# A stated order for ScalarE and VectorE in layer zero's attention, and softmax in two steps

## The chip, the cores and the metric

The kernel runs on one core of one Trainium2 chip. The metric is the device time of one execution in microseconds (us). Five engines run beside each other, each through its own list of instructions in order, and they meet at semaphores: TensorE (PE in the profile; its weight loads are PEld), VectorE (DVE), ScalarE (ACT), GpSimd (POOL) and SyncE (SP), whose queue issues the transfers.

## The reference, cut to what matters

A decoder trunk of two layers on 256 tokens of width 1024 (two tiles of 128 tokens). Each layer mixes, then runs a dense feed-forward part (FFN).

```
xn = rms_norm(h, norm_mix[i]);  mn = rms_norm(mem, norm_mem[i])
q, k, v, qm = split(xn @ w_in[i])        # 12 self heads of 64, 4 memory heads
mk, mv = split(mn @ w_mem_kv[i])
self_out = softmax(q k^T / 8 + bias, causal) v   # layer 0: F[t] - F[s], layer 1: ALiBi
mem_out  = softmax(qm mk^T / 8) mv
h = h + concat(self_out, mem_out) @ w_out[i]
h = h + (silu(gate) * up) @ w_down[i]            # of rms_norm(h, norm_ffn[i])
```

In layer 0 F is the running sum of log sigmoid(gate) of each head. With 256 tokens the block selection of layer 1 has no past block, so its heads are causal attention with ALiBi. A last RMSNorm ends it. What the code calls layer 0 is called layer zero below; the change's own words call it layer one.

## The kernel before, in words

All weights come from one stream in the order of use, in units of up to 1 MB, through four `raw` buffers. Each product is computed to near float32 precision from two parts: ScalarE copies half a unit to `hi` in a reduced format (L224) and VectorE subtracts it from the original to give `lo` (L227), a *weight split*; then three matmuls (`prod`, L317) sum hi·hi, lo·hi and hi·lo. There are seven `hi` and seven `lo` buffers. `weights` (L233) asks for a half and has splits emitted up to five halves ahead (`AHEAD`). Activations get the same treatment (`split_ps`, L242: a *head split* where it is a head's output `x_hT`).

A planner at build time orders each engine's instructions by priority, which is the order of emission, and takes the first that its model of the machine has ready. Inside `tc.manual_schedule(engines=...)` the named engines keep the order of emission; where a region's instructions fall among others of the same engine stays the planner's choice. The whole body (L773) is such a region for PE and SP. For ACT and DVE only the v products of layer 0 are (L479), and a last part of layer 1.

A mixer (L466) runs the v products, then three rounds g of queries and keys (`qk_ps`, 96 matmuls each, two pairs of heads a round). Ahead of round 1 come the memory heads (`memory_heads`, L552): in layer 0 first the memory's keys and values (`mem_kv`, L340: products mk and mv, then the spread of the memory's RMS factors over the partitions, `rsb_ps_mem`), then the queries qm. Then the output products `o_acc` follow, in four pieces. The memory's factors need a square over each tile of mem (`factor`, L257: ScalarE `junk_mem` at L254, VectorE, GpSimd); these are emitted in `mem_kv` after its fourth product (L359).

Attention itself is woven in. `attend` (L393) is a generator for a pair of heads; `step()` (L460) moves every live one on to its next `yield`. A step is called after every second k of a round, in mem_kv, in the middle of qm, and ahead of each group of twelve output matmuls. For one pair the stages are: some idle steps (`IDLE`); in one step the bias adds (L543, layer 0), the scores `s` (8 matmuls), the maxima (L415 with the bias for causal heads, called a causal pass here; L418 for memory heads), the exponentials (L425), the reciprocal (L426) and the scaling (L429); two steps later for memory heads, three for causal ones, the transposes `pT` (L436) and their copies (L439 ScalarE, L440 VectorE); two steps later `o` and the head split.

Counted from the first in mem_kv, the steps of layer 0 are: 1 to 4 in mem_kv, 5 in qm, 6 to 9 in round 1, 10 to 13 in round 2, 14 to 19 in the output products, 20 to 22 behind them. With m00 and m01 the memory pairs and s00 to s05 the causal ones, scores come in step 7 (m00), 8 (s00 and m01), 9 (s01), 12 (s02), 13 (s03), 16 (s04), 17 (s05); transposes in step 9 (m00), 10 (m01), 11, 12, 15, 16, 19, 20 (s00 to s05). Matmul outputs go to eight PSUM banks in rotation, and a stage waits until a bank is read out. Probabilities and their transposes share the tag `probs` with three buffers; the two tiles of mem use it at the start.

The change and the prediction's steps touch attend, mixer, mem_kv, the FFN's `spread` (L669) and the tiles of mem (L163).

## Time and profile before

| | |
|---|---|
| median of 3 runs | 624.39 us (624.07 to 624.49) |
| profiled execution | 623.77 us, span 622.0 us |
| mean granted TensorE clock | 0.998 |
| TensorE busy | 608.5 us, 98% of the span |
| VectorE, ScalarE busy | 455.8 us, 392.4 us |

The span goes from the first to the last instruction of the profiled execution. A busy time counts overlapping instructions once. Waits of an engine are marked with what ended them, which is inferred from semaphores; the end of a matmul is modelled.

### The profile page before, as it was taken

To read this page: it belongs to the slowest core of one execution; us is meant where nothing else is said; L and a number is where in the kernel's file an instruction comes from. 1 tells how busy PE (TensorE), PEld (TensorE's weight loads), DVE (VectorE), ACT (ScalarE), POOL (GpSimd) and SP (SyncE) were. 2 spreads that over 40 slices of the span, in tenths; PEclk is the share of its full clock that TensorE was granted. 3 is DMA by queue.
4 is the path that set the end of the run, shared out by engine and by line. 5 is a ranking of instruction groups with operands and counts; after the bars stand their busy time and mean duration, and the time that the engine had idled before them with its cause. 6 is when DMAs were issued, how large, how long until landed. Compare 5 with 4: busy or idle time off the path is not lost.

```text
span 622.0 us, 9564 instructions
## 1 busy us (share of the span) xinstructions
PE 608.5 (98%) x3640; PEld 533.9 (86%) x3640; DVE 455.8 (73%) x827; ACT 392.4 (63%) x737; POOL 61.6 (10%) x90
## 2 busy tenths in 40 slices
PE   8999999999999999999999999999999999999995
PEld 6999887788888888888899999877888888888884
DVE  5677999978677676678675679986867666666664
ACT  7879788575555555557467589865755555555542
POOL 2023122046000000000011032200000000000000
PEclk9999999999999999999999999999999999999999
DMA  8977431525455545555455642332455555555301
GB/s 354 420 276 273 169 136 69 202 96 214 174 195 204 193 173 184 194 203 190 165 187 203 243 144 89 136 135 99 155 191 199 204 188 173 184 199 203 136 1 67
DMA packets 16774, 112.31 MB, mean 181 GB/s; under 512 B 1996, under 2 KB 2008, under 8 KB 4312
## 3 DMA queue, kind: packets, MB, share of 16 engines
q1 hardware_dynamic: 16440, 111.42, 49.1%
q8 instruction: 28, 0.46, 0.3%
q10 hardware_dynamic: 288, 0.29, 0.1%
q14 instruction: 18, 0.15, 0.1%
HBM read 110.64 MB, written 1.06 MB: 180 GB/s over the span
## 4 chain that ended last, share of the span: by engine, by line
PE 81%; DVE 9%; ACT 7%; issue 1%; DMA 1%; SPq 0%; POOLq 0%; POOL 0%; DVEq 0%
PE gu L180 40%; PE d_acc L180 18%; PE qk_ps L180 6%; PE o_acc L180 5%; PE v_ps L180 5%; DVE lo L227 2%; ACT hi L224 2%; DMA raw<-in_stream 1%; PE s_s L180 1%; PE mv_ps L180 1%; PE qm_ps L180 1%; PE mk_ps L180 1%; DVE p_s L415 1%; PE o_s L180 1%; DVE p_s L429 1%
## 5 line engine op out<-in xcount | busy, mean ns | idle before, releaser
L227 DVE TENSOR_TENSOR lo<-raw,hi 128x1024 fp32r<-128x1024 f32 (+3 forms) x201 | 241.0, 1206 | 69.1 <-ACT hi L224 63.8
L224 ACT ACTIVATE hi<-raw 128x1024 fp32r<-128x1024 f32 (+3 forms) x201 | 206.4, 1035 | 73.5 <-PE d_acc L180 47.0
L180 PE MATMUL gu<-x_ffn,hi 128*128 128x512 f32 x704 | 177.5, 392 | 0.0
L180 PEld LDWEIGHTS gu<-x_ffn,hi 128*128 128x128 f32 x704 | 126.3, 189 | 22.2
L180 PE MATMUL d_acc<-hi,h 128*128 128x512 f32 x348 | 107.1, 389 | 0.0
L180 PEld LDWEIGHTS gu<-x_ffn,lo 128*128 128x128 f32 x704 | 96.7, 190 | 8.1 <-ACT x_ffn L248 1.0
L180 PE MATMUL gu<-x_ffn,lo 128*128 128x256 f32 x704 | 100.5, 284 | 0.1
L180 PEld LDWEIGHTS d_acc<-hi,h 128*128 128x128 f32 x348 | 65.3, 188 | 13.6
L180 PE MATMUL qk_ps<-x_x,hi 128*128 128x256 f32 x384 | 72.4, 284 | 0.9 <-ACT p_m L425 0.9
L180 PE MATMUL d_acc<-lo,h 128*128 128x512 f32 x174 | 67.7, 389 | 0.0
L180 PEld LDWEIGHTS qk_ps<-x_x,hi 128*128 128x128 f32 x384 | 60.9, 191 | 1.9 <-ACT p_m L425 1.1
L180 PE MATMUL qk_ps<-x_x,lo 128*128 128x256 f32 x192 | 54.3, 283 | 0.0
L675 ACT ACTIVATE gate<-gu 128x256 f32<-128x256 f32 x44 | 16.9, 384 | 57.6 <-PE gu L180 57.6
L180 PE MATMUL o_acc<-hi,x_hT 128*128 128x512 f32 x128 | 41.7, 405 | 0.5 <-DVE x_hT L246 0.5
L675 ACT ACTIVATE up<-gu 128x256 f32<-128x256 f32 x44 | 16.9, 385 | 39.6 <-PE gu L180 39.4
L180 PEld LDWEIGHTS d_acc<-lo,h 128*128 128x128 f32 x174 | 32.7, 188 | 6.7
L676 DVE TENSOR_TENSOR gate<-gu,gate 128x256 f32<-128x256 f32 x44 | 18.6, 423 | 25.5 <-ACT gate L675 25.5
L180 PEld LDWEIGHTS qk_ps<-x_x,lo 128*128 128x128 f32 x192 | 36.8, 191 | 0.0
L676 DVE TENSOR_TENSOR up<-gu,up 128x256 f32<-128x256 f32 x44 | 18.7, 424 | 24.6 <-ACT up L675 24.6
L180 PE MATMUL v_ps<-hi,x_x 128*128 128x384 f32 (+1 forms) x128 | 33.2, 339 | 0.1
L425 ACT ACTIVATE p_s<-p_s,nmax_s 128x128 f32<-128x128 f32 (+1 forms) x48 | 21.3, 445 | 11.4 <-DVE nmax_s L415 11.4
L180 PEld LDWEIGHTS o_acc<-hi,x_hT 128*128 128x128 f32 x128 | 22.7, 188 | 6.2 <-DVE x_hT L246 1.2
(155 smaller groups left out, 753.7 us busy)
## 6 DMA issues: line engine op xcount, KB each, us to landing
raw<-in_stream SPq DMA_DIRECT2D x94, 1024.0 KB, 4.8
raw<-in_stream SPq DMA_DIRECT2D x3, 1036.0 KB, 7.8
raw<-in_stream SPq DMA_DIRECT2D x4, 768.0 KB, 5.1
fk<-fd SPq DMA_DIRECT2D x3, 512.0 KB, 7.1
raw<-in_stream SPq DMA_DIRECT2D x2, 518.0 KB, 4.2
h<-in_x SPq DMA_DIRECT2D x2, 512.0 KB, 11.9
mem<-in_mem SPq DMA_DIRECT2D x2, 512.0 KB, 12.8
gfin<-in_norm_final SPq DMA_DIRECT2D x1, 512.0 KB, 3.5
```

The source lines that it names most:

```text
L180: nc.tensor.matmul(o, lhsT, rhs, start=self.fresh, stop=stop, skip_group_check=True)
L224: nc.scalar.activation(hi[:, c0:c1], src[:, c0:c1], AF.Copy)
L227: nc.vector.tensor_sub(lo[:, c0:c1], src[:, c0:c1], hi[:, c0:c1].bitcast(F32))
L415: nc.vector.tensor_tensor_reduce(pr[:, a, c], sb[a].t[:, c], more[qt][:, a], scale=-1.0, scalar=-NEG, op0=ALU.add, op1=ALU.min, accum_out= ...
L425: nc.scalar.activation(pr[:, a, c], src, AF.Exp, bias=nmax[:, a, j], scale=scale, accum_out=total[:, a, j])
L429: nc.vector.tensor_scalar_mul(pr[:, a, c], pr[:, a, c], rc[:, a, qt:qt + 1])
L675: nc.scalar.activation(v[:, 1], b[s].t[:, S:], AF.Copy)
L676: nc.vector.tensor_add(v[:, 0], b[s].t[:, :S], v[:, 1])
```

## The change

Five edits:

1. In layer 0 rounds 1 and 2 of queries and keys, each with the steps it calls and the scaling and splitting of queries and keys behind it, and then the output products up to the last step are regions in which ACT and DVE keep the order of emission. The memory heads between are not. Layer 1 stays with the planner.
2. In attend (both layers) the bias is emitted one step earlier, and the reciprocal with the scaling one step later than the exponentials (that step is taken from the ones before the transposes). One reciprocal over four columns replaces two over two.
3. Softmax, the copies of transposes and the head splits get a priority of 75 places (`URGENT`) ahead of their place of emission. Inside the new regions the order of emission holds all the same.
4. The memory's factors are emitted behind round 0, ahead of the x spread, not in mem_kv.
5. `probs` has four buffers, and the FFN's spread factor shares the buffer of the mixer's (tag `x` for `f`).

```diff
+URGENT = 75
-    mem_t = [ap.tile([P, 2, 512], F32, tag="probs", name=f"mem{t}", bufs=3)...
+    mem_t = [ap.tile([P, 2, 512], F32, tag="probs", name=f"mem{t}", bufs=4)...
...
-                if i == 0 and k == 3:
-                    rs_mem.extend(factor(mem_t[t], f"mem{t}") for t in range(NT))
...
-        for _ in range(idle):
+        for _ in range(idle - 1):
             yield
         if causal:
             more = bias(h0)
+        yield
         sb = [bank(f"s_{name}_{a}") for a in range(2)]
...
+        with tc.high_priority(offset=URGENT):
             for a in range(2):
                 for qt in range(NT):
...                 # maxima (L415, L418)
             for a in range(2):
                 for qt in range(NT):
...                 # exponentials (L425)
-            nc.vector.reciprocal(rc[:, a], total[:, a])
-            for qt in range(NT):
-                c = slice(qt * S, qt * S + nk[qt] * P)
-                nc.vector.tensor_scalar_mul(pr[:, a, c], pr[:, a, c], rc[:, a, qt:qt + 1])
-        for _ in range(SOFTMAX_STEPS[causal]):
+        yield
+        with tc.high_priority(offset=URGENT):
+            nc.vector.reciprocal(rc.rearrange("p a t -> p (a t)"), total.rearrange("p a t -> p (a t)"))
+            for a in range(2):
+                for qt in range(NT):
+                    c = slice(qt * S, qt * S + nk[qt] * P)
+                    nc.vector.tensor_scalar_mul(pr[:, a, c], pr[:, a, c], rc[:, a, qt:qt + 1])
+        for _ in range(SOFTMAX_STEPS[causal] - 1):
             yield
...
+        with tc.high_priority(offset=URGENT):
             nc.scalar.activation(pT[:, 0, :width], tb[0].t[:, :width], AF.Copy)
             nc.vector.tensor_copy(pT[:, 1, :width], tb[1].t[:, :width])
...
+        with tc.high_priority(offset=URGENT):
             split_ps(dst[0][:, kt, :], dst[1][:, kt, :], ob.t[:, :S])
...
         for g in range(3):
             if g == MEM_AT[i]:
                 memory_heads()
+            with tc.manual_schedule(engines={ACT, DVE}) if g >= MEM_AT[i] and i == 0 else nullcontext():
                 kb = [bank(f"qk_ps{i}{2 * g + a}") for a in range(2)]
...             # the round's products, with a step() behind every second k
+                if i == g == 0:
+                    rs_mem.extend(factor(mem_t[t], f"mem{t}") for t in range(NT))
                 if g == 0:
                     rsb = spread(rs, f"x{i}", (DH ** -0.5, 1.0), "x")
...             # queries and keys of two pairs, their attend() started
+        with tc.manual_schedule(engines={ACT, DVE}) if i == 0 else nullcontext():
             acc = [[bank(f"o_acc{i}{t}{c}") for c in range(2)] for t in range(NT)]
...
             for n, j in enumerate((3, 0, 1)):
                 for kk in range(2):
                     step()
                     for t in range(NT):
                         o_item(n, j, kk, t)
             while active:
                 step()
...
-                rsb.append(spread(rs, f"f{i}", (1.0,), "f")[:, 0])
+                rsb.append(spread(rs, f"f{i}", (1.0,), "x")[:, 0])
```

## Rows read from the trace of the kernel before

**Rows 1.** From the page: the span, and busy time, share and instructions of each engine.

```profile
span 622.0 us, 9564 instructions
...
PE 608.5 (98%) x3640; PEld 533.9 (86%) x3640; DVE 455.8 (73%) x827; ACT 392.4 (63%) x737; POOL 61.6 (10%) x90
```

**Rows 2.** Busy time by stretch: the stretch and its length, then busy us and, in brackets, instructions of PE, PEld, DVE, ACT and POOL in this order, the granted clock of TensorE, the share of time in which the DMA engines are busy, and GB/s.

```profile
24.00:62.00 38.00, 37.11 (x305) 36.12 (x304) 29.00 (x41) 33.45 (x63) 8.93 (x9) 1.00 0.77 300
62.00:124.00 62.00, 59.03 (x408) 49.94 (x407) 60.08 (x174) 45.49 (x119) 10.02 (x16) 1.00 0.39 144
124.00:130.00 6.00, 5.93 (x33) 4.76 (x33) 3.88 (x8) 2.77 (x6) 0.00 (x0) 1.00 0.05 18
367.00:425.00 58.00, 57.20 (x404) 49.09 (x403) 50.62 (x148) 44.15 (x119) 8.75 (x15) 1.00 0.41 145
```

**Rows 3.** Timeline of TensorE in layer zero's heads: start, duration, line, operation, output <- inputs, and in brackets the idle time ahead of it with what ended it.

```profile
62.21 0.62 PE L180 MATMUL s_m<-mk,xqm 128*128 128x256 f32 x3
...
74.45 0.39 PE L180 MATMUL qk_ps<-x_x,hi 128*128 128x256 f32 x1 [0.88 <-ACT p_m L425]
...
77.33 0.86 PE L436 MATMUL pT_m<-sq,p_m 128*128 128x128 f32 x5 [0.46 <-DVE nmax_s L415]
...
103.17 0.50 PE L180 MATMUL s_s<-xk,xq 128*128 128x256 f32 x2 [1.01 <-DVE pT_s L440]
...
123.01 0.50 PE L180 MATMUL o_acc<-hi,x_hT 128*128 128x512 f32 x1 [0.30 <-DVE x_hT L246]
```

**Rows 4.** Timeline of TensorE around the two spreads, the one of x ahead of mk and the one of mem ahead of qm.

```profile
35.13 0.28 PE L180 MATMUL qk_ps<-x_x,hi 128*128 128x256 f32 x1
...
35.61 0.36 PE L180 MATMUL mk_ps<-x_mem,hi 128*128 128x256 f32 x1
...
48.70 0.28 PE L180 MATMUL mv_ps<-lo,x_mem 128*128 128x256 f32 x1
...
50.60 0.36 PE L180 MATMUL qm_ps<-x_x,hi 128*128 128x256 f32 x1
```

**Rows 5.** ScalarE: from the timeline, the first copy of the x spread with the idle time ahead of it; from the chain of work that ended last, the squares over mem.

```profile
35.89 0.38 ACT L280 ACTIVATE rsb_x<-rsb_ps_x 128x256 f32<-128x256 f32 x1 [3.22 <-PE rsb_ps_x L180]
...
47.41 2.08 ACT junk_mem L254 x4
```

**Rows 6.** The transfers of mem: their issue on SP's queue, and in the list of issues their size and the median time to landing in us.

```profile
17.89 0.90 SPq L196 DMA_DIRECT2D mem<-in_mem  x2
...
mem<-in_mem SPq DMA_DIRECT2D x2, 512.0 KB, 12.8
```

**Rows 7.** Timeline of VectorE at two places of layer zero.

```profile
101.43 1.23 DVE L227 TENSOR_TENSOR lo<-raw,hi 128x1024 fp32r<-128x1024 f32 x1
102.57 0.55 DVE L440 COPY pT_s<-pT_s 128x384 f32<-128x384 f32 x1
...
121.41 1.22 DVE L227 TENSOR_TENSOR lo<-raw,hi 128x1024 fp32r<-128x1024 f32 x1
122.54 0.42 DVE L246 TENSOR_TENSOR x_hT<-o_s,x_hT 128x256 fp32r<-128x256 f32 x1
```

**Rows 8.** Timeline of VectorE and ScalarE: the last of m00's maxima, and the hi that follows m00's exponentials.

```profile
66.63 0.41 DVE L418 TENSOR_REDUCE nmax_m<-s_m 128x1 f32<-128x256 f32 x1
...
68.23 1.07 ACT L224 ACTIVATE hi<-raw 128x1024 fp32r<-128x1024 f32 x1
```

**Rows 9.** VectorE's groups of instructions from 62 to 124 us, one for each form: line, operation, output <- inputs, count | busy us, mean ns | idle time ahead of them in us.

```profile
L227 DVE TENSOR_TENSOR lo<-raw,hi 128x1024 fp32r<-128x1024 f32 x15 | 18.5, 1245 | 0.1
L543 DVE SCALAR_TENSOR_TENSOR fk<-fk,fq,sq 128x256 f32<-128x256 f32 x12 | 5.4, 472 | 0.0
L415 DVE CUSTOM_DVE_ANT_0 p_s<-s_s,fk 128x256 f32<-128x256 f32 x12 | 5.0, 415 | 0.0
...
L543 DVE SCALAR_TENSOR_TENSOR bias<-fk,fq,sq 128x128 f32<-128x128 f32 x12 | 3.8, 340 | 0.0
...
L415 DVE CUSTOM_DVE_ANT_0 p_s<-s_s,bias 128x128 f32<-128x128 f32 x12 | 3.4, 281 | 0.0
...
L418 DVE TENSOR_REDUCE nmax_m<-s_m 128x1 f32<-128x256 f32 x8 | 3.0, 409 | 0.0
...
L429 DVE TENSOR_SCALAR p_m<-p_m,rc_m 128x256 f32<-128x256 f32 x8 | 2.4, 341 | 0.0
L382 DVE TENSOR_TENSOR xq<-qk,xq 64x256 fp32r<-64x256 f32 x4 | 2.3, 579 | 0.3 <-ACT xq L380 0.2
L391 DVE TENSOR_TENSOR xk<-qk,xk 64x256 fp32r<-64x256 f32 x4 | 2.1, 529 | 0.1
```

**Rows 10.** Timeline of TensorE and VectorE in layer one.

```profile
385.30 1.09 PE L180 MATMUL o_m<-pT_m,mv 128*64 128x256 f32 x8 [0.64 <-ACT pT_m L439]
...
421.98 1.22 DVE L227 TENSOR_TENSOR lo<-raw,hi 128x1024 fp32r<-128x1024 f32 x1
...
423.58 0.50 PE L180 MATMUL o_acc<-hi,x_hT 128*128 128x512 f32 x1 [0.16 <-DVE x_hT L246]
```

**Rows 11.** Timeline of GpSimd and VectorE where both subtract, and of VectorE alone.

```profile
84.12 1.44 POOL L382 TENSOR_TENSOR xq<-qk,xq 64x256 fp32r<-64x256 f32 x1 [2.90 <-ACT xq L380]
84.99 0.85 DVE L382 TENSOR_TENSOR xq<-qk,xq 64x256 fp32r<-64x256 f32 x1
...
100.99 0.42 DVE L391 TENSOR_TENSOR xk<-qk,xk 64x256 fp32r<-64x256 f32 x1
```

## The prediction

> **What bounds the kernel now.** The profiled execution took 623.77 us for a span of 622.0 us, 0.62 us below the median of 624.39 us; the sum is made on the 623.77, and the difference is added back at the end. I read the page's first part first: TensorE is busy 608.5 of 622.0 us [rows 1], so a change of order can win only what TensorE waits for. Then the busy time by stretch, which compares the two attention stages [rows 2]. From 62 to 124 us, layer zero's heads, VectorE is busy 60.08 of 62 us and TensorE loses 2.97; in the same part of layer one, 367 to 425 us, VectorE is busy 50.62 of 58 and TensorE loses 0.80. Before that, from 24 to 62 us, ScalarE is the fuller of the two, 33.45 of 38. So layer zero is limited first by ScalarE and then by VectorE, layer one by TensorE. TensorE's granted clock is 1.00, the upper level, in each of these stretches [rows 2].

> Last the timeline of TensorE, which names the waits one by one. From step 7 on, which begins with the memory heads' first scores at 62.21, the marked ones are 0.88 us (a bank that m01's exponentials still read), 0.46 (a bank of s01's scores), 1.01 (a copy of probabilities) and 0.30 (the last head's split) [rows 3]. Ahead of these stands the spread of the memory factors. From the last mv product (48.70) to the first qm product (50.60) pass 1.90 us; the same four spreading matmuls in front of mk take from 35.13 to 35.61, 0.48 us [rows 4].

> **Part 1, the memory factors earlier.** The two squares of mem take ScalarE 2.08 us at 47.41 [rows 5]. The change emits them ahead of the x spread. There ScalarE is idle for 3.22 us up to 35.89 [rows 5], and mem, issued from 17.89 and landing 12.8 us later, is there at 31 [rows 6]. The squares fit, the factors are ready some 12 us before TensorE wants them, and 1.90 - 0.48 = 1.42 us go. The other end is 0 (the planner leaves the squares late). I take -1.4, since the idle stretch is there and nothing else is asked of it. It also frees 2.08 us of ScalarE in its full stretch, so that splits and queries reach VectorE earlier at 60 us.

> **Part 2, the late waits of layer zero.** The wait at 103.17 is for a probability copy begun at 102.57, and ahead of that copy VectorE did a weight split at 101.43 [rows 3, 7]. The wait at 123.01 is for the head split at 122.54, behind a weight split at 121.41 [rows 3, 7]. In stated order the copy of step 15 stands ahead of the next weight split, and the head splits of steps 21 and 22 have none between them. Both go: 1.01 + 0.30 = 1.31. The other end is 0, another wait in their place. I take -1.3: in both the operation in front is one that the order moves.

> **Part 3, the early steps in stated order.** Here order costs. A split needs ScalarE's hi before VectorE's lo, and the hi now stands behind the exponentials of the step before it. At the memory heads' maxima VectorE ends the last one at 67.04 (66.63 + 0.41); ScalarE, which then still has exponentials to do, comes to a hi at 68.23 and ends it at 69.30 [rows 8]. In the kernel before VectorE fills these 2.26 us with other work; in emission order it stands still, once in step 7 and once in step 8. Now the work itself. VectorE's starts come some 0.08 us before the end of the operation ahead (121.41 + 1.22 against 122.54 [rows 7]), so from the mean durations [rows 9]: a lo 1.16; four maxima 1.29; a causal pass over two sizes twice, 1.08; four bias adds 1.29; the four scalings of a memory head with a reciprocal 1.11, those of a causal head taken as much; a copy 0.5 [rows 7]. From step 7 on the order is lo, bias s00, maxima m00, hole, lo, pass s00, bias s01, scale m00, maxima m01, hole, lo, scale s00, pass s01, copy m00, scale m01: 14.6 us of work and 4.5 of holes. TensorE wants m01 scaled when it transposes it in step 10, now at 77.33, 15.1 us after step 7 began, 13.8 without the two waits of 1.34 [rows 3]. VectorE is taken to be free when step 7 begins. So at worst 5.3 us of waiting take the place of 1.34, +4.0; at best all of it goes, -1.34, because copies no longer queue for one of three buffers and banks come free sooner. Without a hole it is 14.6 against 13.8, -0.5; with one of the two 16.9, +1.8. The planner may fill a hole with the next region's split, since only the order inside a region is fixed. I take +0.8, between these last two and nearer the hole, since the holes follow from the order itself.

> **Part 4, layer one.** Only priority acts here: softmax operations rank 75 emitted instructions earlier. TensorE waits 0.64 us at 385.30 for a ScalarE copy of probabilities and 0.16 at 423.58 for a head split that follows a weight split at 421.98 [rows 10]. Both may go, 0.80; the other end is one weight split pushed into TensorE's way, +1.2 [rows 9]. I take -0.5, more than half of the gain, as splits have five halves of lead.

> **Costed at nothing.** One reciprocal for two saves an instruction in each of eight heads, at most 0.6 us of VectorE, which reaches the path only through Part 3. Stated look-ahead is five halves where seven buffers let the planner run one or two further; two splits, 2.3 us of VectorE, move behind 124 us, where it is busy 3.88 of 6 us [rows 2]. That cover gone, 1.2 us each. The FFN's factor in the buffer of x's: the last head's scaling reads that long before the FFN writes it; a wait there would cost the spread once, 0.5 us a layer [rows 4]. The extra yields leave TensorE's stages where they are: bias a step earlier, scaling a step later, transposes unmoved. SP's queue keeps its order and no transfer is added; DMA is busy 0.39 of the stretch [rows 2].

> **Sum.** -1.4 - 1.3 + 0.8 - 0.5 = -2.4: 623.77 to 621.4, and the median 624.39 to 622.0 us.

> **Rivals.**
> *All waits go.* Parts 1 and 2 whole and half of the best of Parts 3 and 4: -1.42 - 1.31 - 0.67 - 0.40 = -3.8, 620.6 us. For it: each wait of layer zero is for softmax or a split. Against: VectorE is full there.

> *A wait for a wait.* Part 3 at its worst: -1.4 - 1.3 + 4.0 - 0.5 = +0.8, 625.2 us. For it: both holes are in the order as written. Against: the planner's freedom between regions.

> *Slower: VectorE's holes decide the whole stretch.* Besides the two of 2.26 there is one wherever exponentials stand right ahead of a split: about 0.97 in steps 12 and 16, where bias adds cover 1.29 of it, and 2.26 in step 17; 8.7 in all. Less two splits (2.3) and the reciprocals (0.6) that is 5.8, of which VectorE's idle time takes 1.9 [rows 2]: +3.9, less Parts 1 and 4, +2.0, 626.4 us. It decides if VectorE's lateness after step 10 is still there at the copies of the last heads, from step 19 on.

> *Ports.* Queries and keys of four heads are eight VectorE subtractions; if each takes 0.85 as at 84.99 and not 0.42 as at 100.99, that is 3.4 us, of which the means of 579 and 529 ns already hold 1.07 [rows 9, 11]. 2.4 more eat up the gain: 624.4 us. At 84.99 GpSimd is inside a subtraction begun at 84.12 [rows 11]. [...] Against: ScalarE's copies of queries come one after the other, so the two engines start apart.

> **Chances.** Forecast 0.34, all waits go 0.13, a wait for a wait 0.27, slower 0.22, ports 0.04. A difference of 0.2%, 1.25 us, is about what a measurement of this kernel can tell from none. Faster 0.47, same 0.31, slower 0.22. The forecast alone spans 621.0 to 623.1. The range of 620.2 to 626.8 leaves out the better third of the second case and the worse half of the fourth.

> **What would show it.** Part 1: squares near 33 us, and under 0.6 us from the last mv to the first qm product. Part 2: no wait at the second scores of s04 nor at the last output piece. Part 3: VectorE idle ahead of two lo splits after the memory heads' maxima, and a wait of TensorE ahead of m01's transposes, 2 us if I am right in part. Part 4: none for o_m in layer one. The forecast is wrong if VectorE shows several holes of 2 us between 62 and 120 us that TensorE shares, or if the waits of steps 9 and 10 vanish as well.

## The result, and the profile after

The changed kernel takes 632.75 us (median of 4 runs, 632.03 to 633.20) against 624.23 us of the kernel before (4 runs, 623.93 to 624.49): a ratio of 1.0136, 95% interval 1.0118 to 1.0153. It is 8.5 us slower, beyond the range given and with the other sign. The profiled execution took 633.20 us, with a span of 631.4 us against 622.0 [rows 1]. The reading below accounts for these 9.4 us.

The span and the busy time of each engine, from the page of after:

```profile
span 631.4 us, 9538 instructions
PE 613.7 (97%) x3640; PEld 538.1 (85%) x3640; DVE 456.8 (72%) x811; ACT 393.1 (62%) x737; POOL 62.6 (10%) x90
```

The same work, except for 16 reciprocals; yet TensorE is busy 5.2 us longer. The busy time by stretch, columns as in [rows 2]:

```profile
24.00:62.00 38.00, 37.85 (x312) 37.05 (x311) 29.02 (x42) 35.05 (x63) 8.80 (x10) 1.00 0.82 315
62.00:124.00 62.00, 54.47 (x354) 46.99 (x353) 52.04 (x149) 38.42 (x109) 9.13 (x15) 0.92 0.28 104
367.00:425.00 58.00, 57.69 (x430) 51.67 (x430) 51.63 (x143) 49.34 (x130) 15.98 (x20) 1.00 0.38 133
```

Layer zero's heads carry the loss: VectorE is busy 52.04 us where it was 60.08, so it stands still for 10 of 62 us; TensorE waits 7.5 us instead of 3.0; and a new thing, its granted clock is 0.92 there instead of 1.00. The two stretches beside it are better than before. TensorE's waits one by one, from its timeline:

```profile
61.50 1.21 PE L181 MATMUL s_m<-mk,xqm 128*128 128x256 f32 x8 [0.15 <-POOL xqm L381]
73.58 1.52 PE L440 MATMUL pT_m<-sq,p_m 128*128 128x128 f32 x8 [2.29 <-DVE p_m L433]
75.99 0.58 PE L181 MATMUL qk_ps<-x_x,hi 128*128 128x256 f32 x1 [0.89 <-ACT p_m L426]
83.50 1.24 PE L440 MATMUL pT_m<-sq,p_m 128*128 128x128 f32 x8 [2.08 <-DVE p_m L433]
110.02 1.18 PE L181 MATMUL s_s<-xk,xq 128*128 128x256 f32 x8 [0.66 <-DVE pT_s L445]
115.81 0.90 PE L181 MATMUL s_s<-xk,xq 128*128 128x256 f32 x5 [1.04 <-DVE pT_s L445]
117.27 0.62 PE L181 MATMUL s_s<-xk,xq 128*128 128x256 f32 x3 [0.56 <-DVE xk L390]
126.21 0.51 PE L181 MATMUL o_acc<-hi,x_hT 128*128 128x512 f32 x1 [0.83 <-DVE x_hT L247]
132.00 0.50 PE L181 MATMUL o_acc<-hi,x_hT 128*128 128x512 f32 x1 [0.17 <-DVE x_hT L247]
```

The first two large ones wait for the scaling of m00 and m01 (`p_m`, L433). What holds the scaling up shows in the timeline of VectorE, and below it in that of ScalarE:

```profile
65.36 1.41 DVE L419 TENSOR_REDUCE nmax_m<-s_m 128x1 f32<-128x256 f32 x4
69.05 1.23 DVE L228 TENSOR_TENSOR lo<-raw,hi 128x1024 fp32r<-128x1024 f32 x1 [2.29 <-ACT hi L225]
...
74.13 1.41 DVE L419 TENSOR_REDUCE nmax_m<-s_m 128x1 f32<-128x256 f32 x4
77.83 1.23 DVE L228 TENSOR_TENSOR lo<-raw,hi 128x1024 fp32r<-128x1024 f32 x1 [2.29 <-ACT hi L225]
...
79.06 1.19 DVE L228 TENSOR_TENSOR lo<-raw,hi 128x1024 fp32r<-128x1024 f32 x1
...
83.00 1.14 DVE L433 TENSOR_SCALAR p_m<-p_m,rc_m 128x256 f32<-128x256 f32 x4
```

```profile
67.50 0.48 ACT L426 ACTIVATE p_m<-s_m,nmax_m 128x256 f32<-128x256 f32 x1
...
67.95 1.07 ACT L225 ACTIVATE hi<-raw 128x1024 fp32r<-128x1024 f32 x1
```

After the maxima of m00 VectorE's next instruction is a lo. Its hi stands on ScalarE behind the four exponentials that these maxima release, so VectorE idles 2.29 us; m01's maxima bring the same again. These are the two holes of Part 3, predicted at 2.26. At 79.06 another split comes ahead of m01's scaling. It stands between the reciprocal of s00 (78.98) and its scaling (80.18), which follow each other in the order of emission, so it is from outside the region: the planner's freedom lengthened the chain here by 1.1 us.

The clock, in the busy time of short stretches:

```profile
62.00:71.30 9.30, 9.29 (x79) 9.09 (x77) 6.91 (x18) 3.66 (x12) 0.95 (x3) 1.00 0.33 126
71.30:76.00 4.70, 1.53 (x9) 1.02 (x9) 4.14 (x15) 2.17 (x11) 0.61 (x2) 0.83 0.63 223
76.00:81.40 5.40, 5.40 (x24) 5.18 (x24) 3.57 (x10) 2.74 (x6) 0.00 (x0) 0.52 0.07 17
81.40:84.50 3.10, 1.02 (x9) 0.89 (x9) 3.06 (x14) 2.34 (x9) 0.00 (x0) 1.00 0.77 309
84.50:89.00 4.50, 4.50 (x28) 4.50 (x27) 3.36 (x9) 4.00 (x8) 1.70 (x2) 0.62 0.00 0
```

TensorE worked for 1.53 of the 4.70 us up to 76.00, and the granted clock fell: it is 0.83 there and 0.52 over the next stretch, where 24 matmuls fill 5.4 us. It is 1.00 over the next 3.10 us, 0.62 over the 4.50 us behind the wait of 2.08, and 1.00 again from 89 to 627 us.

**The account.** Step 7 begins 0.71 us earlier than before (61.50 against 62.21 [rows 3]). From there to the first product of the FFN (129.00 us before, 138.70 after) TensorE's marked waits are 5.26 in steps 7 to 10 (1.34 before) and 3.26 behind them (1.63 before, with one of 0.32 at 108.44): +3.92 and +1.63. What the lower clock adds to TensorE's busy time is an estimate, busy time multiplied by one less the clock in the rows above: 0.26 + 2.59 + 1.71 = 4.6. From the first product of this FFN to that of the next one pass 300.93 us (439.63 - 138.70) instead of 301.23 (430.23 - 129.00): -0.30. The sum is -0.71 + 3.92 + 1.63 + 4.6 - 0.30 = 9.1 of the 9.4 us. That these are causes and not just places is what the experiments are for.

### The profile page after: what moved, and what is told of

It is laid out like the page before. It is cut to its first block, busy times and chain, and to the rows that moved or that the text cites. A ratio compares the mean times of both kernels' runs of the same rounds, so it can differ in the third digit from the quotient of the medians.

```text
span 631.4 us, 9538 instructions
## 1 busy us (share of the span) xinstructions
PE 613.7 (97%) x3640; PEld 538.1 (85%) x3640; DVE 456.8 (72%) x811; ACT 393.1 (62%) x737; POOL 62.6 (10%) x90
## 4 chain that ended last, share of the span: by engine, by line
PE 83%; DVE 9%; ACT 5%; issue 1%; POOL 0%; POOLq 0%; DVEq 0%; ACTq 0%
PE gu L181 39%; PE d_acc L181 18%; PE qk_ps L181 8%; PE v_ps L181 5%; PE o_acc L181 4%; DVE lo L228 3%; ACT hi L225 2%; PE s_s L181 1%; PE mv_ps L181 1%; PE qm_ps L181 1%; PE mk_ps L181 1%; DVE p_s L416 1%; PE pT_s L440 1%; PE warm_ps L181 1%; DVE p_s L433 1%
## 5 line engine op out<-in xcount | busy, mean ns | idle before, releaser
L228 DVE TENSOR_TENSOR lo<-raw,hi 128x1024 fp32r<-128x1024 f32 (+3 forms) x201 | 240.2, 1201 | 74.6 <-ACT hi L225 69.5
L181 PE MATMUL qk_ps<-x_x,hi 128*128 128x256 f32 x384 | 75.8, 293 | 0.9 <-ACT p_m L426 0.9
L181 PEld LDWEIGHTS qk_ps<-x_x,hi 128*128 128x128 f32 x384 | 63.9, 201 | 2.1 <-ACT p_m L426 1.3
L181 PE MATMUL qk_ps<-x_x,lo 128*128 128x256 f32 x192 | 56.1, 292 | 0.0
L686 ACT ACTIVATE gate<-gu 128x256 f32<-128x256 f32 x44 | 16.9, 384 | 57.5 <-PE gu L181 57.5
L686 ACT ACTIVATE up<-gu 128x256 f32<-128x256 f32 x44 | 16.9, 385 | 39.8 <-PE gu L181 39.5
L181 PEld LDWEIGHTS qk_ps<-x_x,lo 128*128 128x128 f32 x192 | 38.6, 201 | 0.0
```

Source lines behind the costliest of these rows:

```text
L181: nc.tensor.matmul(o, lhsT, rhs, start=self.fresh, stop=stop, skip_group_check=True)
L228: nc.vector.tensor_sub(lo[:, c0:c1], src[:, c0:c1], hi[:, c0:c1].bitcast(F32))
L686: nc.scalar.activation(v[:, 1], b[s].t[:, S:], AF.Copy)
```

## The experiments

My theory (A in the expectations): the order of emission in the stated rounds puts ScalarE's hi behind exponentials; VectorE's holes make its scaling late, and the rest follows. The rivals: another edit costs it and not the order; the order costs, but by something other than the holes, or in the output's region; the lower clock makes a good part of it. Medians, with ratios to the kernel before, measured beside each of them (624.0 us each time):

| kernel | us | ratio, 95% interval |
|---|---|---|
| no stated order | 621.95 | 0.9964 (0.9951 to 0.9977) |
| stated order in the output alone | 624.39 | 1.0007 (0.9998 to 1.0016) |
| in round 2 and the output | 626.31 | 1.0038 (1.0024 to 1.0051) |
| in the two rounds alone | 633.28 | 1.0158 (1.0137 to 1.0179) |
| all, lo one split later | 625.70 | 1.0024 (1.0015 to 1.0033) |
| all, hi ahead of the exponentials | 626.87 | 1.0052 (1.0040 to 1.0065) |
| lo later, order in the rounds alone | 624.59 | 1.0008 (0.9999 to 1.0017) |
| all, filler matmuls | 631.28 | 1.0120 (1.0105 to 1.0136) |
| lo later, filler matmuls | 626.46 | 1.0044 (1.0031 to 1.0057) |
| before, early memory factors | 625.07 | 1.0012 (1.0003 to 1.0022) |
| the same, copies of pT with priority | 622.97 | 0.9981 (0.9972 to 0.9991) |
| no stated order, no priority | 624.37 | 1.0008 (0.9999 to 1.0016) |

### Where the stated order costs

All five edits but the first, nothing in stated order:

```diff
-with tc.manual_schedule(engines={ACT, DVE}) if g >= MEM_AT[i] and i == 0 else nullcontext():
+with nullcontext():
...
-with tc.manual_schedule(engines={ACT, DVE}) if i == 0 else nullcontext():
+with nullcontext():
```

> The changed kernel without its new regions: ScalarE and VectorE of layer zero's attention go back to the planner; the memory factors early, the softmax in two steps, the priority and the fourth buffer stay. Theory A (the stated order makes the holes and so the loss): the two idle stretches of 2.29 us ahead of VectorE's lo disappear, TensorE waits under 1.5 us ahead of the memory heads' transposes, and the time is 622 to 624.5 us, at or a little below the kernel before. Rival B (two-step softmax itself brings the scaling of m01 too late, whatever the order): TensorE still waits over 3 us there and the time stays above 628 us.

Measured 621.95 us, just under what the theory said: the stated order alone costs 10.8 us, and the rest of the change is a gain of 2.0. All marked waits in TensorE's timeline from 62 to 124 us, and then the busy time of this stretch:

```profile
73.16 0.39 PE L181 MATMUL qk_ps<-x_x,hi 128*128 128x256 f32 x1 [1.06 <-ACT p_m L426]
96.95 1.07 PE L440 MATMUL pT_s<-sq,p_s 128*128 128x128 f32 x6 [0.52 <-DVE nmax_s L416]
120.89 0.50 PE L181 MATMUL o_acc<-hi,x_hT 128*128 128x512 f32 x1 [0.18 <-DVE x_hT L247]
```

```profile
62.00:124.00 62.00, 60.17 (x411) 50.46 (x410) 58.14 (x166) 44.20 (x118) 9.46 (x15) 1.00 0.37 138
```

VectorE is busy 58.14 of the 62 us, the clock is at 1.00, and of the waits of before [rows 3] that ahead of m01's transposes and the 1.01 us at 103.17 are gone. This kernel beats both.

The second of the two lines of the diff alone (order in the rounds only):

> The changed kernel with the regions of the two rounds of queries and keys only; the output products go back to the planner. Theory A, with the holes of steps 7 and 8 as the main cost: 630 to 632 us, since about 7 of the 8.5 us are lost before 90 us. Rival (the loss is spread over the whole stretch, as holes at steps 12 to 17 too): 627 to 629 us.

Measured 633.28 us, 1.3 above the upper end of what the theory said and not to be told from the whole change: with the rounds in stated order, that of the output adds nothing.

The first line alone (order in the output only):

> Edit: the two rounds (steps 6 to 13) go back to the planner, the output's region (steps 14 to 19) keeps the stated order, all else as after. Theory A (the stated order costs only where a softmax with its exponentials stands in one step with the split of the next weights, in the rounds): near the kernel with no stated order at all, 621.5 to 624.0 us. Rival B (the output's waits of 0.66, 1.04, 0.56 and 0.83 us in the trace of after come from the stated order there too): 624.5 to 627.

Measured 624.39 us, just above the 624.0 of theory A and just below rival B's 624.5, so it lies between them. Against no stated order the output's region does cost 2.4 us where the rounds are the planner's. It has a hole of its own, in step 17 (VectorE's timeline), and a wait of TensorE behind it (TensorE's); ahead of it TensorE waits 0.46, 0.42 and 0.55 us for copies and a head split, which no stated order does not have:

```profile
115.43 1.23 DVE L228 TENSOR_TENSOR lo<-raw,hi 128x1024 fp32r<-128x1024 f32 x1 [1.98 <-ACT hi L225]
```

```profile
117.04 0.50 PE L181 MATMUL o_acc<-hi,x_hT 128*128 128x512 f32 x1 [0.83 <-DVE x_hT L247]
```

Round 1 alone back to the planner:

```diff
-if g >= MEM_AT[i] and i == 0
+if g > MEM_AT[i] and i == 0
```

> Edit: round 1 (steps 6 to 9) goes back to the planner, round 2 and the output keep the stated order. Theory A (each softmax of memory heads in a stated round opens its own hole of 2.29 us on VectorE): about half of the loss comes back, 626 to 629 us, one hole ahead of a lo. Rival B (the order of round 1 starts all of it, and round 2 only hands it on): 624 or less.

Measured 626.31 us, inside theory A's numbers but for another reason than the one given. Both memory heads take their maxima in steps 7 and 8, which belong to round 1; so neither hole of 2.29 us is left; the longest are one of 0.62 at 85.30 and the one of 1.98 in step 17. From no stated order: +2.4 for the output, +1.9 for round 2, +6.4 for round 1. Round 1 is the costliest. The three parts hold only in this order of adding: behind the rounds in stated order the output's adds nothing, as the run with the rounds alone shows.

### What in round 1

Inside the regions each lo is issued behind the next split's hi, one split later:

```diff
-            nc.vector.tensor_sub(lo[:, c0:c1], src[:, c0:c1], hi[:, c0:c1].bitcast(F32))
+            for f in late_lo:
+                f()
+            late_lo.clear()
+            late_lo.append(lambda c0=c0, c1=c1: nc.vector.tensor_sub(lo[:, c0:c1], src[:, c0:c1], hi[:, c0:c1].bitcast(F32)))
+            if not lag[0]:       # outside the regions: at once
+                late_lo.pop()()
```

> The changed kernel, with one thing different inside the regions: VectorE's lo of a weight split is emitted behind ScalarE's hi of the next split, one split later. VectorE then never waits for a hi that stands behind exponentials; its work is the same. Theory A (the holes): idle time ahead of lo from 69.5 us of waits for hi down by 4.6 us around 60 to 80 us, TensorE's waits ahead of m00's and m01's transposes down from 4.7 us to under 1.5, and 625 to 628 us. Rival C (not the holes but the amount of VectorE's work that stands ahead of the scaling): 631 us or more, the waits about as long.

Measured 625.70 us: 7.05 of the loss go, with every instruction and the rest of the order kept. VectorE goes from the maxima straight into a lo whose hi is long there, and TensorE's wait for m00's scaling is gone; that for m01 is 1.80, with the clock at 0.66 over the 5 us behind it. So the theory's time came out, but its waits did not: 4.37 us (not 4.7) became 1.80, with 0.35 more for a bank between the two, where it said under 1.5. Of the 1.80, 1.1 are again a split from outside the region: at 75.46 it stands between m01's reciprocal and its scaling (76.58). VectorE's timeline, TensorE's, and the busy time behind the wait:

```profile
70.08 1.41 DVE L426 TENSOR_REDUCE nmax_m<-s_m 128x1 f32<-128x256 f32 x4
71.40 1.22 DVE L233 TENSOR_TENSOR lo<-raw,hi 128x1024 fp32r<-128x1024 f32 x1
```

```profile
77.07 1.60 PE L447 MATMUL pT_m<-sq,p_m 128*128 128x128 f32 x8 [1.80 <-DVE p_m L440]
```

```profile
77.00:82.00 5.00, 4.93 (x28) 4.82 (x29) 4.80 (x12) 3.16 (x8) 1.45 (x2) 0.66 0.00 0
```

From the other side: in the rounds the next split is issued between a softmax's maxima and its exponentials.

```diff
+            if weave[0]:         # in the rounds
+                split()
             total = sp.tile([P, 2, NT], F32, tag="total", name=f"total_{name}")
```

> Edit: in the stated rounds the split of the next weights is issued between a softmax's maxima and its exponentials, so that ScalarE makes hi ahead of the exponentials and VectorE's lo follows its maxima at once; all else as after. Theory A (the holes are VectorE's wait for a hi that stands behind exponentials): no hole of 2 us ahead of a lo at 66 to 78 us, and 624.5 to 627 us, as with lo issued one split later. Rival C (the stated order costs by something else, and lo one split later helped by moving other work): 630 or more.

Measured 626.87 us, with no hole above 0.5 us ahead of a lo before step 17. VectorE's timeline at m01's maxima, in an execution of 628.30 us:

```profile
72.80 1.41 DVE L421 TENSOR_REDUCE nmax_m<-s_m 128x1 f32<-128x256 f32 x4
74.13 1.22 DVE L230 TENSOR_TENSOR lo<-raw,hi 128x1024 fp32r<-128x1024 f32 x1
```

TensorE still waits 1.20 and 1.95 us for p_m. Two different edits that both take the hole away bring back 5.9 and 7.05 us, so the rival that all of the order's cost is something else falls: the holes are the cause of most of the loss. Against no stated order 4.9 and 3.75 us are left. Of the 3.75, 1.1 are the output's order (next run); the rest is not taken apart.

Lo one split later, and the output back to the planner:

```diff
-        with tc.manual_schedule(engines={ACT, DVE}) if i == 0 else nullcontext():
+        lag[0] = False
+        with nullcontext():
             acc = [[bank(f"o_acc{i}{t}{c}") for c in range(2)] for t in range(NT)]
```

> Edit: lo one split later in the stated rounds, and the output (steps 14 to 19) back to the planner. Theory A (the output's stated order costs 2.4 us of its own wherever the rounds hand over in time, 624.39 against 621.95 us): 622.8 to 624.2 us. Rival B (it costs nothing once the rounds are in stated order, as 633.28 against 632.75 us has it): 625.2 to 626.3 us.

Measured 624.59 us, between the two: the output's order is worth 1.1 us here by the medians (the 95% intervals just overlap), 2.4 where rounds 1 and 2 are the planner's, nothing where the holes are left. A reading that no run tests: the later VectorE already is, the less one more wait costs.

### The clock

18 short bfloat16 matmuls ahead of the transposes of m00 and of m01 keep TensorE at work while it waits; the transposes overwrite what they write.

```diff
+        if name in ("m00", "m01"):
+            for _ in range(FILL):
+                nc.tensor.matmul(tb[0].t[:, :2 * P], ident.bitcast(BF16)[:, :P], ident.bitcast(BF16), start=True, stop=True, ...)
```

> The changed kernel with 18 small bf16 matmuls ahead of the transposes of each of m00 and m01, into the bank that the transposes then overwrite; they keep TensorE occupied while it waits for VectorE. Theory D (TensorE's granted clock falls after the waits, and the fall behind the second one is exposed): the granted clock stays at 1.0 from 71 to 89 us where it was 0.52 and 0.62, and the time falls by 1.5 to 2.5 us to 630.3 to 631.3. Rival (VectorE sets the pace and hides the slow clock): clock up, time within 0.5 us of 632.75.

Measured 631.28 us, 1.5 less than after, with more work in the queue. The clock stays at 1.00 in the busy time of both stretches, where after had 0.52 and 0.62:

```profile
76.00:81.40 5.40, 2.94 (x24) 2.60 (x23) 4.01 (x12) 2.73 (x7) 0.00 (x0) 1.00 0.08 23
...
84.50:89.00 4.50, 4.50 (x38) 3.82 (x38) 3.35 (x9) 4.33 (x10) 1.50 (x3) 1.00 0.01 4
```

The 24 matmuls take 2.94 us instead of 5.40, and TensorE spends what it saved on waiting for m01, whose chain on VectorE is no shorter. TensorE's timeline:

```profile
83.32 1.04 PE L444 MATMUL pT_m<-sq,p_m 128*128 128x128 f32 x8
```

Step 7 begins at 61.07 here, so m01's transposes come 22.25 us behind it; in after it is 22.00 (83.50 - 61.50). So of the 4.6 us estimated for the lower clock about 1.5 reach the end, those behind 84.50; the first fall hides behind VectorE's chain. A lower clock as the main cause is ruled out.

The same filler where lo comes one split later:

> Edit: lo one split later in the stated regions, and 18 short matmuls ahead of the transposes of m00 and of m01 each, whose result the transposes overwrite, so that TensorE works while it waits for them. Theory A (behind the wait of 1.80 us at 77.07 us the lower clock costs some 1.5 us in that kernel): 624.0 to 624.8 us with the clock at 1.00 from 76 to 82 us. Rival B (VectorE decides there and the clock is hidden): 625.2 to 626.2 us.

Measured 626.46 us, 0.8 slower, just outside rival B's numbers and no test of what it was made for. The clock is at 1.00 from 70.65 to 82 us, but each filler takes 2.14 us, and ahead of m00 there was hardly a wait to hide it: 4.3 us of filler replace waits of 2.15 (1.80 and the 0.35 for a bank). TensorE's timeline:

```profile
70.65 2.14 PE L447 MATMUL pT_m<-sq 128*128 128x256 bf16 x18
...
76.38 2.14 PE L447 MATMUL pT_m<-sq 128*128 128x256 bf16 x18
```

How time and clock go together in that kernel shows in its ten executions without filler. Five of them, with a mean granted clock of 0.997, took 624.67 to 625.31 us; the other five, at 0.994 and 0.995, took 626.09 to 626.29. So 1.3 us between the medians of the two groups (624.87 and 626.18) go with the clock, near theory A's 1.5, and the filler costs more than it saves. That the clock makes them is not shown: with hi ahead of the exponentials an execution at 0.998 took 626.61 us and one at 0.994 took 626.48.

### The early factors, and the priority

The kernel before with edit 4 alone:

```diff
-                if i == 0 and k == 3:
-                    rs_mem.extend(factor(mem_t[t], f"mem{t}") for t in range(NT))
...
+            if i == g == 0:
+                rs_mem.extend(factor(mem_t[t], f"mem{t}") for t in range(NT))
```

> Edit: the kernel before with one part of the change alone, the memory's factors early (junk_mem ahead of the spread of rsb_x). By the prediction's sum: the 1.42 us wait between mv and qm goes, 1.2 to 1.4 us less, 622.6 to 622.8 us. Rival: the wait comes back behind, where TensorE next waits for the softmax of m00 (0.88 and 0.46 us in before): 623.4 to 624.2 us.

Measured 625.07 us (11 runs, 623.47 to 625.96): slower, beyond what either side had. Step 7 does begin 0.93 earlier, at 61.28. Then the gain is eaten up: the waits in steps 9 and 10 are 1.11 and 0.88 (0.88 and 0.46 before [rows 3]), and at 103 us the planner, with other ready times, puts ScalarE's copy of pT_s behind the splits of the next keys. ScalarE's timeline, TensorE's, and the busy time behind the wait:

```profile
102.50 0.41 ACT L387 ACTIVATE xk<-qk 64x256 fp32r<-64x256 f32 x1
102.82 0.47 ACT L437 ACTIVATE pT_s<-pT_s 128x384 f32<-128x384 f32 x1
```

```profile
103.43 1.98 PE L180 MATMUL s_s<-xk,xq 128*128 128x256 f32 x8 [1.98 <-ACT pT_s L437]
```

```profile
104.00:106.00 2.00, 2.00 (x8) 1.68 (x7) 1.97 (x4) 1.69 (x3) 0.00 (x0) 0.50 0.99 418
106.00:108.00 2.00, 2.00 (x7) 1.55 (x6) 2.00 (x11) 0.59 (x3) 0.00 (x0) 0.68 0.00 0
```

Behind a wait of 1.98 us the clock is 0.50 for 2 us and 0.68 for 2 more; by the same estimate that adds 2 x 0.50 + 2 x 0.32 = 1.6 us.

The same kernel, and the change's priority on the two copies of pT:

```diff
+        with tc.high_priority(offset=75):
             nc.scalar.activation(pT[:, 0, :width], tb[0].t[:, :width], AF.Copy)
             nc.vector.tensor_copy(pT[:, 1, :width], tb[1].t[:, :width])
```

> Edit: the kernel before with the memory's factors early (as in the run of that part alone, 625.07 us) and with the change's priority on the two copies of pT alone. Theory A (the part alone lost its 1.2 us and more because the planner then put ScalarE's copy of pT_s behind the splits of the next keys, 102.82 us in that trace against 100.41 in before: TensorE waits 1.98 us there, and its clock is at half for some 3 us behind it): the wait at 103 us is under 1.1 us, the clock stays at 1.00, 622.0 to 623.3 us. Rival B (something else in the early factors costs): 624.5 us or more.

Measured 622.97 us, as A had it: 2.1 us less, faster than before. The copy is done at 100.3, and TensorE's timeline marks no wait from 76 to 116 us. ScalarE's timeline, and the busy time of an earlier stretch:

```profile
99.81 0.49 ACT L438 ACTIVATE pT_s<-pT_s 128x384 f32<-128x384 f32 x1
```

```profile
76.00:82.00 6.00, 6.00 (x44) 6.00 (x44) 5.91 (x21) 5.78 (x17) 1.87 (x3) 0.80 0.00 0
```

That the clock would stay at 1.00 was wrong: it is 0.80 in this stretch, behind the waits of 1.10 and 0.88. In the run of the early factors alone it is 1.00 there, behind 1.11 and 0.88:

```profile
76.00:82.00 6.00, 6.00 (x51) 5.66 (x52) 5.69 (x22) 5.77 (x18) 2.27 (x3) 1.00 0.00 0
```

The change with neither stated order nor priority (this edit at all four places, beside those of the first experiment):

```diff
-        with tc.high_priority(offset=URGENT):
+        with nullcontext():
```

> Edit: the change with neither stated order nor priority: early factors, softmax in two steps, fourth buffer, biases one step earlier. Theory A (with no stated order, the priority is what keeps the gain of the early factors): 624.0 to 625.5 us, as with the early factors alone. Rival B (the two steps and the fourth buffer make it): 621.5 to 622.5 us, as with the priority.

Measured 624.37 us, as A had it: of what the change brings without the order, 2.4 us hang on the priority; without it two-step softmax, biases earlier and a fourth buffer stand 0.7 us below the early factors alone (625.07), with overlapping intervals, and win nothing against before.

## Why the prediction was wrong, step by step

**Part 3 is the step that failed: the holes and VectorE's chain were taken at +0.8 and cost 6.9 us, 3.9 of them as waits of TensorE.** The two holes are there, 2.29 us each where 2.26 was said, and the order of VectorE's work is the one given. I took +0.8, between no hole and one, because the planner might fill a hole with the next region's split. But both holes lie inside round 1, and the split that the planner did move, at 79.06, came behind them and ahead of m01's scaling: it filled nothing and lengthened the chain. The rows said two holes, and nothing in them said half of one.

The worst case of Part 3 was too small as well. It had m01's transposes 19.1 us behind the start of step 7; they came 22.00 behind it (83.50 - 61.50), 15.12 before (77.33 - 62.21), so +6.88. VectorE was not free when step 7 began, as Part 3 takes it: its lo starts at 62.65, 1.15 later. The split at 79.06 is 1.1 more. That TensorE's waits, 5.26 us, match the 5.3 of the worst case is luck: TensorE's own work up to these transposes took 3.0 us longer than before, 2.85 of it by the estimate for the lower clock, and so it waited less for a chain that was longer.

**The lower clock was in no term, nor in a rival.** All stretches of before showed 1.00 [rows 2], and I priced a longer wait of TensorE at its own length. By the estimate in the account it adds 4.6 us to TensorE's busy time; 2.85 of them run beside VectorE's chain and are in the 6.88, and 1.71 come on top, of which the filler run brought back 1.5.

**Part 2 read the order wrongly.** It let the copies and head splits come ahead of the weight split in front of them. In after a lo still ends right ahead of the copies at 109.33 and 115.11, with waits of 0.66 and 1.04 behind: that lo was issued one step earlier in the program, and a stated order cannot pass it. A lo also ends ahead of the last head split (131.53), with a wait of 0.17 behind. In the region none stands between the two, as Part 2 says, but the planner put one there from behind the region. VectorE's timeline at the first and the last of these places:

```profile
108.19 1.22 DVE L228 TENSOR_TENSOR lo<-raw,hi 128x1024 fp32r<-128x1024 f32 x1
109.33 0.55 DVE L445 COPY pT_s<-pT_s 128x384 f32<-128x384 f32 x1
...
130.40 1.22 DVE L228 TENSOR_TENSOR lo<-raw,hi 128x1024 fp32r<-128x1024 f32 x1
131.53 0.75 DVE L247 TENSOR_TENSOR x_hT<-o_s,x_hT 128x256 fp32r<-128x256 f32 x2
```

What takes the wait for a copy away is the priority, with the planner free to use it, as the run with early factors and priority shows. In place of -1.3 the stretch from step 11 on has +1.6, with 0.83 of its waits behind the hole in step 17, which no part had.

**The terms together.** Part 1 came to -0.71 for -1.4, Part 2 to +1.63 for -1.3, Part 3 to +6.88 for +0.8, Part 4 to -0.30 for -0.5, and the lower clock behind m01 to +1.71 for nothing: 9.2 for -2.4, of 9.4 measured on the profiled executions.

**Part 1 was right as a wait.** The squares run at 33.00 and 34.04 and the spread follows mv without a gap (timelines of ScalarE and of TensorE):

```profile
33.00 1.05 ACT L255 ACTIVATE junk_mem<-mem 128x1024 bf16<-128x1024 f32 x1
```

```profile
49.12 0.28 PE L181 MATMUL mv_ps<-lo,x_mem 128*128 128x256 f32 x1
...
49.60 0.36 PE L181 MATMUL qm_ps<-x_x,hi 128*128 128x256 f32 x1
```

0.48 us from the last mv to the first qm product, the price of the spread [rows 4]. As a term of the sum it was too large: 0.71 reached step 7 (0.42 of the rest was lost ahead of it: TensorE's first queries and keys begin at 24.15, in before at 23.73), and alone it brought nothing.

**Part 4** had the sign: -0.30 where -0.5 was taken. The wait at 385.30 of 0.64 [rows 10] has become this one in TensorE's timeline, and the one for the last head split is left, with 0.17 at 433.01:

```profile
390.26 1.25 PE L440 MATMUL pT_m<-sq,p_m 128*128 128x128 f32 x8 [0.31 <-DVE p_m L433]
```

**The rivals.** The slower one had the mechanism and the main places: holes at steps 7, 8 and 17 (1.98 there, 2.26 said). Those of 0.97 in steps 12 and 16 did not come (0.42 and none), and its condition, VectorE still late at the copies of the last heads, does not show: the last copies that TensorE waits for are those of s02 and s03 (110.02 and 115.81). At 626.4 us it was 6.3 short. It let VectorE's spare time absorb 1.9 of the holes and charged TensorE with nothing more than VectorE's lateness. The subtractions of the rival on ports add little: VectorE's four queries take a mean of 786 ns (579 before [rows 9]), the four keys 422 (529), +0.4 us together. The three long ones of after again began inside a subtraction of GpSimd, 0.84 us at 90.45 (GpSimd from 89.54), 0.95 at 107.22 (from 107.15) and 0.93 at 112.61 (from 112.53); one of the same size with GpSimd idle took 0.42 (109.91). No run shows that GpSimd makes them long, nor that ports do.

## What to carry to other kernels

When two engines are put in a stated order, follow each pair in which one feeds the other (here hi on ScalarE, lo on VectorE) and look what stands ahead of the feeding half: if it is released by the consumer's previous instruction, the consumer idles for all of it (2.29 us here, twice), and issuing the dependent half one turn later takes that away. Here this brought back 7.05 of the 10.8 us that the order costs; dropping the order brought back all of them. A region does not keep the planner from putting work of its own choice between two of its instructions, as at 79.06. Where a hole follows from the order as written, take it whole into the sum, and ask whether the consumer is free when the chain begins. A wait taken away is a gain only if the next ones don't grow, so test an early step together with the priority that keeps its gain.
